# The last two up pairs product by product, both convolutions inside the first down product, activation loads first

## The chip, the cores and the metric

One NeuronCore of one Trainium2 chip. The metric is the device time of one execution in microseconds, the median of several runs. The kernel before: 1073.26 us (median of 3 runs, 1072.83 to 1077.39).

## What is computed

One decoder layer on 1024 positions of width 1024, in fp32. The change lies in its last third, the gated MLP with a causal depthwise convolution of width 3:

```python
h = rmsnorm(x, ffn_norm_g[l])
up = causal_depthwise_conv(h @ w_up[l], conv_w[l], conv_b[l])
a, bgate = jnp.split(up, [D_FF], axis=-1)
x = x + (jax.nn.silu(a) * bgate) @ w_down[l]
...
return rmsnorm(x, final_norm_g)
```

D_FF is 2816, which is 22 tiles of 128 rows for each of the two halves of `up`.

## The kernel before, in words

**Two-part numbers.** A TensorE product of an fp32 matrix is made of three: both operands are split into a high part (`...h`, made by ACT, line 113 for weights and 842 for activations of the down product) and the rest (`...l`, a subtraction on DVE, lines 114 and 843), and h·h, h·l and l·h are added up.

**Up pairs.** A `Unit` takes two column tiles of `w_up`, tile i and tile 22 + i (`wa` and `wb`; pair 20 is u20 in the trace), and computes both with seven products of half size instead of eight (Strassen's scheme in Winograd's form). Each product is 12 matmuls of 128x512 (line 146). The right-hand operands R11, R21, T1, T2, R22, T3, T4 lie split on the chip. The weights of the products are `a` (the raw tile), `b` (sums s), `c` (sums t) and `d` (half a raw tile); `prep_a`, `sums_s`, `split_s`, `sums_t`, `split_t` and `prep_b` make them (the sums: line 159), and `p(k)` issues product k and then what reads it from PSUM (`n1` to `n7`, lines 204 to 246). Products 1, 2, 5, 6, 3, 7, 4 accumulate in PSUM tiles X, Z and Y; from them come `ra` and `rb`, the pair's two rows of `up`. Product 7's sum must be read from X (`n7`, DVE) before product 4 adds to X.

**Convolution.** `conv` makes three taps for ra and three for rb (ACT for the first, lines 789 and 798 with the silu; DVE for two each, lines 790 and 791) and the gate, a product on DVE (line 800; on POOL for the first two pairs). The tiles are named cv. `blocks_of(j)` (POOL, lines 804 to 812) then writes seven combinations of the gated tiles of two pairs to `gb` in DRAM: plain copies and differences.

**Down product.** It has the same form: seven products over blocks of half size, in the order SEQ = 2, 1, 5, 6, 3, 7, 4, each over 11 tiles (22 pairs, two by two) and four row tiles p, so 4 x 33 = 132 matmuls (line 883). Product 2 goes to dZ, 1, 6 and 7 to dX, 5 and 3 to dY. `load_act(i, j)` fetches a pair of tiles from `gb` (g20 to g24 for product 2, g10 to g14 for product 1, and so on) and splits them; `load_wt(i, t)` fetches a weight tile of `w_down` (wd20 to wd25 for product 2) and splits it, for products 5, 6, 3 and 7 after a sum or difference with another. The last of the 11 tiles of products 2 and 1 does not come through `gb`: it is split from the gated tile on the chip (g2e and g1e). dZ is therefore issued without its last tile first, and with it at the end.

**What sets the order.** Engines run their instructions in order; a scheduler of the framework sets the order on each from the source's order and its own estimates. In blocks marked `manual_schedule` for PE, TensorE's order is that of the source. Raw weights of pairs and of the down product share four buffers (tag w); the split high and low parts of weights rotate over three buffers each (wh, wl). SP starts nearly all loads, POOL the stores of `gb`. Before the change, TensorE's manual block begins at dZ (line 981): the last pair, 21, runs alone by `pair(last, ahead)`, which calls the convolution of pair 20 and the loads of product 2 between its products, and the scheduler places the first matmuls of dZ between pair 21's.

Of the kernel before, what the change touches and what calls it, by code (L numbers as in the profile page):

```python
# [12 lines left out]
AF = mybir.ActivationFunctionType  # L13
ALU = mybir.AluOpType
# [3 lines left out]
S = 1024  # L18
# [5 lines left out]
FT = FF // P  # L24
# [3 lines left out]
KH = FT // 2  # L28
# [37 lines left out]
def decoder_layer(ctx, tc, io, out):  # L66
    nc = tc.nc
# [8 lines left out]
    def U(name, dt=F32, shape=(P, 1024)):  # L76
        return up.tile(list(shape), dt, tag="u", name=name)
# [21 lines left out]
    def V(key, j=None):  # L99
        o, n = VEC[key]  # L100
        return vec[:, o:o + n] if j is None else vec[:, o + j:o + j + 1]
# [49 lines left out]
    class Unit:  # L151
        def __init__(u, ws, R, name, tile=W, kh=4):
            u.wa, u.wb = ws
            u.kh = kh
            u.a = [u.wa[:, o:o + kh] for o in (0, kh)] if not isinstance(u.wa, list) else u.wa
            u.R, u.name, u.tile = R, name, tile
# [4 lines left out]
        def prep(u, src, key, eng=None):  # L161
            h, l = split_w(src, u.name + key, eng=eng)
            return [(h[:, o:o + u.kh], l[:, o:o + u.kh]) for o in range(0, src.shape[1], u.kh)]
# [105 lines left out]
    def unit(srcs, R, name):  # L269
        u = Unit(load_pair(srcs, name), R, name)  # L270
        u.prep_a()
        u.p(1)
        u.p(2)
        return finish(u)
# [11 lines left out]
    def both(us, *names):  # L286
        for n in names:
            for u in us:
                u.p(n) if isinstance(n, int) else getattr(u, n)()
# [29 lines left out]
    R = {k: [] for k in ("R11", "R21", "T1", "T2", "R22", "T3", "T4")}  # L319
# [143 lines left out]
    for half in range(2):  # L463
        ps = M(f"r1bc{half}")
# [34 lines left out]
    for h in range(NH):  # L499
# [10 lines left out]
        for half in range(2):  # L510
            ps = small4(f"pS{h}{half}", lambda o, j: nc.tensor.matmul(o, kT[:, cut(half * 4 + j)], qT[:, cut(half * 4 + j)], start=True, stop=True))
# [14 lines left out]
        for n in range(NCH - 1):  # L526
            src = pkv[n // 4][:, n % 4]
# [27 lines left out]
        g = h  # L555
        ws, cb = hc[:, 2], hc[:, 3]
# [8 lines left out]
        if g:  # L565
            svT, u = unit([io["w_in"][:, 20 + g], io["w_in"][:, 16 + g]], R, f"G{g}")
        else:
            g0.wb = W("G0w1")
            nc.sync.dma_start(g0.wb, io["w_in"][:, 16])
            svT, u = finish(g0)  # L570
# [58 lines left out]
    R = {}  # L629
# [8 lines left out]
    class Out:  # L638
# [28 lines left out]
        def all(u):  # L667
            for f in (u.product, u.residual, u.square, u.add):
                f()
# [30 lines left out]
    us = u0, u1 = [Unit(load_pair([io["w_up"][:, i], io["w_up"][:, FT + i]], f"u{i}", UW), R, f"u{i}", UW) for i in range(2)]  # L700
# [83 lines left out]
    gbs = [dp.tile([P, 7, n, HALF], F32, name=f"gb{n}") for n in (KH - 1, 1)]  # L784
    halves = lambda t: t.rearrange("p (a b) -> p a b", b=HALF)

    def taps(r, i):
        t = U(f"cv{i}")
        nc.scalar.activation(t, r, AF.Identity, scale=V("cw", 88 + i), bias=V("cb", i))
        nc.vector.scalar_tensor_tensor(t[:, 1:], r[:, :S - 1], V("cw", 44 + i), t[:, 1:], ALU.mult, ALU.add)  # L790
        nc.vector.scalar_tensor_tensor(t[:, 2:], r[:, :S - 2], V("cw", i), t[:, 2:], ALU.mult, ALU.add)  # L791
        return t

    g = {}

    def conv(ra, rb, i):
        a = taps(ra, i)
        nc.scalar.activation(a, a, AF.Silu)  # L798
        b = taps(rb, FT + i)
        (nc.gpsimd if i < 2 else nc.vector).tensor_tensor(a, a, b, ALU.mult)  # L800
        g[i] = halves(a)


    def blocks_of(j):
# [18 lines left out]
    SEQ = [2, 1, 5, 6, 3, 7, 4]  # L823
# [4 lines left out]
    act = {i: [] for i in SEQ}  # L828
# [3 lines left out]
    def load_act(i, j):  # L832
        n = min(2, KH - 2 * j)
        src = gbs[0][:, BLK[KEY[i]], 2 * j:2 * j + 2] if n == 2 else gbs[1][:, BLK[KEY[i]]]
        if n == 2:
            h, l = [U(f"g{i}{j}{x}", F32R, PAIR) for x in "hl"]
        else:
            e = U(f"g{i}{j}e", F32R, PAIR)
            h, l = e[:, :1], e[:, 1:]
        x = l.bitcast(F32)  # L840
        nc.sync.dma_start(x, src)
        nc.scalar.activation(h, x, AF.Copy)
        nc.vector.tensor_tensor(l, x, h.bitcast(F32), ALU.subtract)
        act[i] += [(h[:, m], l[:, m]) for m in range(n)]
# [8 lines left out]
    def load_wt(i, t):  # L853
        lo, n = 8 * t, min(8, NB - 8 * t)
        raw = []
        for m, src in enumerate(SRC[i]):
            raw.append(W(f"wd{i}{t}{m}")[:, :n])
            nc.sync.dma_start(raw[-1], src[:, lo:lo + n])
        w = raw[0]
        if i == 5:  # L860
            sums[t] = U(f"ds{t}", F32, (P, 8, P))
        if i in (5, 6, 3):
            s = sums[t][:, :n]
            x, y, op = {5: (w, raw[-1], ALU.add), 6: (s, w, ALU.subtract), 3: (w, s, ALU.subtract)}[i]
            nc.vector.tensor_tensor(s, x, y, op)  # L865
            w = s
        elif i == 7:
            nc.vector.tensor_tensor(w, w, raw[1], ALU.subtract)  # L868
        h, l = split_w(w, f"wd{i}{t}", tile=(lambda name: U(name, F32R, (P, 8, P))) if i == 2 and t % 2 == 0 or i == SEQ[-1] and t < 4 else None)
        wts[i] += [(h[:, m], l[:, m]) for m in range(n)]  # L870
# [3 lines left out]
    def load_x2(n):  # L874
        x2[n] = U(f"x2{n}")
        nc.sync.dma_start(x2[n], x2d[:, n])

    def down(ps, i, p, start, ks, stop, cols=slice(0, HALF)):
        first = start
        todo = [(k, s) for k in ks for s in range(2)] + [(k, 2) for k in ks]  # L880
        for n, (k, s) in enumerate(todo):
            w, r = wts[i][p * KH + k], act[i][k]
            nc.tensor.matmul(ps, w[s // 2], r[s % 2][:, cols], start=first, stop=stop and n == len(todo) - 1, skip_group_check=True)  # L883
            first = False

    def acc(n, half, ps):
        o = hs(x2[n], half)
        nc.vector.tensor_tensor(o, ps, o, ALU.add)  # L888

    PREP = {2: [(load_act, j) for j in range(5)]}  # L890
    for i in SEQ[1:]:
        PREP[i] = [(f, int(j)) for f, j in zip([load_act, load_act, load_wt] * 3 + [load_wt] * 3, "010231452345")]
        if i == 1:
            PREP[i] = [f for f in PREP[i] if f != (load_act, 5)]

    def prep(i, n):
        for f, j in PREP[i][:n]:
            f(i, j)
        PREP[i] = PREP[i][n:]


    def pair(u, ahead):
        u.p(1)
        ahead(1)
        u.p(2)
        u.sums_s(nc.gpsimd)
        u.split_s()
        ahead(2)
        u.p(5)
        ahead(3)  # L910
        u.p(6)
        u.sums_t(nc.gpsimd)
        u.split_t()
        ahead(4)
        u.p(3)
        u.prep_b()
        ahead(5)
        u.p(7)
        ahead(6)
        u.p(4)  # L920

    for i, (ra, rb) in enumerate(early):
        conv(ra, rb, i)
# [4 lines left out]
        if i % 2:  # L928
            blocks_of(i // 2)

    held = unit([io["w_up"][:, FT - 2], io["w_up"][:, 2 * FT - 2]], R, f"u{FT - 2}")
    last = Up(FT - 1)

    def ahead(j):
        if j == 1:
            conv(*held, FT - 2)
        if j < 6:
            prep(2, 1)
        if j > 2:
            load_wt(2, j - 3)  # L940

    pair(last, ahead)
    for t in range(4, 6):
        load_wt(2, t)
    prep(1, 2)
    conv(last.ra, last.rb, FT - 1)
    load_x2(0)
    load_x2(2)
    e, o = g[FT - 2], g[FT - 1]
# [1 line left out]
    last1 = U("g1e", F32R, PAIR)  # L951
# [26 lines left out]

    ba, bb, bc = Block(HALF, HALF), Block(0, 256), Block(256, 256)
    X = [None] * 4  # L980
    with tc.manual_schedule(engines={mybir.EngineType.PE}):
        Z = [M(f"dZ{p}") for p in range(3)] + [A("dZ3")]
        for p in range(4):
            down(Z[p], 2, p, True, range(KH - 1), False)
            prep(1, 1)
        for p in range(4):
            down(Z[p], 2, p, False, [KH - 1], True)
            if p:
                load_x2(2 * p + 2) if p < 3 else None
            acc(2 * p, 0, Z[p])  # L990
        prep(1, 20)
        act[1].append((last1[:, 0], last1[:, 1]))
        for i, nxt in zip(SEQ[1:-1], SEQ[2:]):
            for p in range(4):
                prep(nxt, 3)
                if i in (1, 6, 7):
                    if i == 1:
                        X[p] = A(f"dX{p}")
                    ps = X[p]
                else:  # L1000
                    if i == 5:
                        load_x2(2 * p + 1)
                    ps = M(f"dY{i}{p}")
                down(ps, i, p, i in (1, 5, 3), range(KH), True)
                for n, half in {1: [(0, 0)], 5: [(0, 1), (1, 1)], 6: [(0, 1)], 3: [(0, 1)], 7: [(1, 1)]}[i]:
                    acc(2 * p + n, half, ps)
                if i == 7:
                    for b in (ba, bb, bc):
                        b.square(2 * p)

    with tc.manual_schedule(engines={mybir.EngineType.PE, mybir.EngineType.DVE, mybir.EngineType.Activation}):
        def squares(b, ns):
# [7 lines left out]
        for k in range(8):  # L1020
            s, p = divmod(k, 4)
# [55 lines left out]
```

## Time and profile before

| | |
|---|---|
| median of 3 runs | 1073.26 us (1072.83 to 1077.39) |
| the profiled execution | 1072.93 us, of which the span is 1071.2 us |
| TensorE busy | 1027.7 us, 96% of the span |
| DVE busy | 826.4 us, 77% |
| ACT busy | 490.7 us, 46% |
| POOL busy | 206.8 us, 19% |
| loads and stores | 141.58 MB, mean 132 GB/s |

A view called the chain follows the execution back from its last instruction, at each step to what released it. The waits say who waited for whom. A timeline lists instructions with their start, their duration and, in brackets, the idle time of the engine before them and what ended it. The windows give busy time per engine, the clock granted to TensorE as a share of full speed, and what the DMA engines did. PE is TensorE's matmuls, DVE VectorE, ACT ScalarE, POOL GpSimd, SP SyncE; buffer numbers are left out of names.

### The profile page before, as it was taken

Reading aid. Unit: us, or ns where it says so; the run is one execution under the profiler, and the core shown is the slowest. Engines: PE = TensorE matmul, PEld = TensorE weight load, DVE = VectorE, ACT = ScalarE, POOL = GpSimd, SP = SyncE. Lnnn points to the kernel's source line nnn. Section 1 sums busy time; section 2 is a strip of 40 time slices with the busy share of each in tenths; the row PEclk is TensorE's granted clock in tenths of the full one; section 3 lists DMA queues with packets and bytes.
Section 4 is the critical chain, followed back from the end, with each engine's and each line's share of the span. In section 5 each row is a group of like instructions: output and inputs, shape, how many; then the busy total and the mean of one; then the engine's idle time right before and its main releaser. Section 6 shows DMA issues by size and latency. Waiting matters only on the chain.

```text
span 1071.2 us, 12690 instructions
## 1 busy us (share of the span) xinstructions
PE 1027.7 (96%) x4794; PEld 849.4 (79%) x4794; DVE 826.4 (77%) x998; ACT 490.7 (46%) x690; POOL 206.8 (19%) x145
## 2 busy tenths in 40 slices
PE   7798999999999999989999999999998899999996
PEld 5586888888888888768888888888887778878896
DVE  7868886958867478998887878878786587886565
ACT  6653444334364353654444534544445444344440
POOL 4602330412210000061123023032123130000000
PEclk9899999999999999999999999999999999999998
DMA  7251031121365240022333233233235678974614
GB/s 286 80 196 40 22 110 62 52 77 62 99 222 191 98 157 20 20 103 98 104 108 103 86 128 118 61 116 119 81 116 177 216 284 296 365 240 161 198 57 158
DMA packets 48446, 141.58 MB, mean 132 GB/s; under 512 B 5056, under 2 KB 9536, under 8 KB 48384
## 3 DMA queue, kind: packets, MB, share of 16 engines
q1 hardware_dynamic: 42752, 120.58, 33.5%
q0 software_dynamic: 5632, 20.19, 4.8%
q8 instruction: 37, 0.61, 0.2%
q14 instruction: 25, 0.20, 0.1%
HBM read 109.03 MB, written 31.72 MB: 131 GB/s over the span
## 4 chain that ended last, share of the span: by engine, by line
PE 73%; DVE 14%; issue 5%; ACT 4%; DMA 2%; POOL 1%; SPq 0%; DVEq 0%; ACTq 0%
PE dX L883 10%; PE po L135 8%; PE dY L883 6%; DVE cv L791 2%; PE A0X L146 2%; PE B0X L146 1%; PE G1X L146 1%; PE A3X L146 1%; PE B3X L146 1%; PE u4X L146 1%; PE u20X L146 1%; DVE cv L790 1%; PE G0X L146 1%; PE B1X L146 1%; DMA wd<-in_w_down 1%
## 5 line engine op out<-in xcount | busy, mean ns | idle before, releaser
L798 ACT ACTIVATE cv<-cv 128x1024 f32<-128x1024 f32 x22 | 23.4, 1062 | 73.5 <-DVE cv L791 73.5
L810 POOL TENSOR_TENSOR cv<-cv 128x512 f32<-128x512 f32 x22 | 38.5, 1752 | 20.8 <-DMA gb<-cv 18.8
L808 POOL DMA_DIRECT2D gb<-cv x11 | 7.9, 715 | 151.0 <-DVE cv L800 150.7
L800 POOL TENSOR_TENSOR cv<-cv,cv 128x1024 f32<-128x1024 f32 x2 | 7.7, 3874 | 140.4 <-ACT u2p L227 140.4
L810 POOL TENSOR_TENSOR cv<-cv,cv 128x512 f32<-128x512 f32 x22 | 31.7, 1442 | 4.8 <-DMA gb<-cv 3.3
L807 POOL DMA_DIRECT2D gb<-cv x11 | 6.5, 589 | 113.8 <-DVE cv L800 113.5
L655 DVE TENSOR_TENSOR xr<-po,xr 128x512 f32<-128x512 f32 x16 | 10.8, 688 | 20.0 <-PE po L135 18.7
L965 ACT ACTIVATE x3q<-x 128x256 f32<-128x256 f32 (+1 forms) x21 | 9.3, 483 | 33.6 <-DVE x L1026 28.3
L800 DVE TENSOR_TENSOR cv<-cv,cv 128x1024 f32<-128x1024 f32 x20 | 24.3, 1216 | 0.1
L661 ACT ACTIVATE xq<-xr 128x512 f32<-128x512 f32 x14 | 8.8, 628 | 24.2 <-DVE xr L655 17.1
L546 ACT ACTIVATE sT<-po 128x128 f32<-128x128 f32 x32 | 8.4, 277 | 13.3 <-PE po L538 13.2
L868 DVE TENSOR_TENSOR wd<-wd,wd 128x1024 f32<-128x1024 f32 (+1 forms) x6 | 6.8, 1136 | 9.7 <-DMA wd<-in_w_down 9.7
L967 DVE TENSOR_TENSOR sq<-sq,x3q 128x256 f32<-128x256 f32 (+1 forms) x20 | 9.8, 516 | 4.2 <-ACT x3q L965 3.8
L976 DVE SCALAR_TENSOR_TENSOR x<-x,vec,r 128x256 f32<-128x256 f32 (+1 forms) x24 | 12.0, 564 | 1.3 <-PE r L622 1.3
L665 DVE TENSOR_TENSOR sq<-sq,xq 128x512 f32<-128x512 f32 x13 | 8.9, 688 | 3.2 <-ACT xq L661 3.1
L675 ACT ACTIVATE nx<-xr,vec 128x512 f32<-128x512 f32 x16 | 10.8, 708 | 0.0
L509 ACT ACTIVATE kn<-pk,vec 128x512 f32<-128x512 f32 x8 | 5.2, 680 | 11.8 <-PE pk L508 11.8
L1026 DVE TENSOR_TENSOR x<-dX,x 128x256 f32<-128x256 f32 x8 | 3.4, 424 | 8.5 <-PE dX L883 8.5
L678 DVE TENSOR_TENSOR nx<-nx,r 128x1024 f32<-128x1024 f32 x8 | 9.5, 1216 | 0.4 <-PE r L622 0.4
L865 DVE TENSOR_TENSOR ds<-wd,wd 128x1024 f32<-128x1024 f32 (+1 forms) x6 | 6.8, 1134 | 3.4 <-DMA wd<-in_w_down 3.4
L336 POOL TENSOR_SCALAR x<-x,vec 128x512 f32<-128x512 f32 x4 | 8.0, 2004 | 7.1 <-DVE R110l L330 7.1
L888 DVE TENSOR_TENSOR x<-dY,x 128x512 f32<-128x512 f32 x12 | 8.1, 685 | 1.1 <-DMA x<-x2d 1.1
(5708 smaller groups left out, 3854.3 us busy)
## 6 DMA issues: line engine op xcount, KB each, us to landing
wd<-in_w_down SPq DMA_DIRECT2D x45, 512.0 KB, 4.4
gb<-cv POOLq DMA_DIRECT2D x33, 512.0 KB, 3.2
wo<-in_w_out SPq DMA_DIRECT2D x10, 512.0 KB, 3.8
x<-in_xT SPq DMA_DIRECT2D x8, 512.0 KB, 8.9
xn<-in_xN SPq DMA_DIRECT2D x8, 512.0 KB, 5.5
xr<-in_xT SPq DMA_DIRECT2D x8, 512.0 KB, 5.9
x2d<-xr SPq DMA_DIRECT2D x8, 512.0 KB, 3.2
x<-x2d SPq DMA_DIRECT2D x8, 512.0 KB, 5.3
```

Of the source, the lines that this page charges most:

```text
L135: nc.tensor.matmul(ps, a, b, start=(k == 0 and t == 0), stop=(k == n - 1 and t == 2))
L146: nc.tensor.matmul(ps, a[:, k], b, start=(start and i == 0), stop=(i == 3 * n - 1), skip_group_check=not start)
L655: nc.vector.tensor_tensor(u.y, u.ps, u.y, ALU.add)
L675: nc.scalar.activation(nx[n // 2][:, n % 2], xr[th][n // 2][:, n % 2], AF.Identity, scale=V("g2", n))
L790: nc.vector.scalar_tensor_tensor(t[:, 1:], r[:, :S - 1], V("cw", 44 + i), t[:, 1:], ALU.mult, ALU.add)
L791: nc.vector.scalar_tensor_tensor(t[:, 2:], r[:, :S - 2], V("cw", i), t[:, 2:], ALU.mult, ALU.add)
L798: nc.scalar.activation(a, a, AF.Silu)
L800: (nc.gpsimd if i < 2 else nc.vector).tensor_tensor(a, a, b, ALU.mult)
L810: nc.gpsimd.tensor_tensor(x, y, z, ALU.subtract)
L883: nc.tensor.matmul(ps, w[s // 2], r[s % 2][:, cols], start=first, stop=stop and n == len(todo) - 1, skip_group_check=True)
L967: nc.vector.tensor_tensor(sq[:, u.blk], sq[:, u.blk], u.t, ALU.add)
L976: nc.vector.scalar_tensor_tensor(y, y, V("gf", n), u.nr.rs, ALU.mult, ALU.mult)
```

## The change

Pairs 20 and 21 are made together: each step is issued for both, one product of the one behind the same product of the other. Their sums s and t go to DVE (before, those of pair 21 were on POOL) and into tiles of the large pool. Both convolutions are called after the last product, so that they lie beside dZ, and TensorE's order is set by hand from pair 20's first product on. The five loads g20 to g24 are started by POOL instead of SP. For product 1 all five activation loads come before its six weight loads; before, each weight followed two activations. The classes and helpers that `taps` is cut into do the same work as before for every other pair.

```diff
+    class Taps:
+        def last(u):
+            u.t = U(f"cv{u.i}")
+            nc.scalar.activation(u.t, u.r, AF.Identity, scale=V("cw", 88 + u.i), bias=V("cb", u.i))
+        def tap(u, d):
+            nc.vector.scalar_tensor_tensor(u.t[:, d:], u.r[:, :S - d], V("cw", 88 - 44 * d + u.i), u.t[:, d:], ALU.mult, ALU.add)
...
     def conv(ra, rb, i):
...
+        a = Taps(ra, i).all()
+        silu(a)
+        gate(i, a, Taps(rb, FT + i).all(), nc.gpsimd if i < 2 else None)
...
-        nc.sync.dma_start(x, src)
+        (nc.gpsimd if i == SEQ[0] else nc.sync).dma_start(x, src)
...
         if i == 1:
-            PREP[i] = [f for f in PREP[i] if f != (load_act, 5)]
+            PREP[i] = [(load_act, j) for j in range(5)] + [(load_wt, j) for j in range(6)]
...
-    held = unit([io["w_up"][:, FT - 2], io["w_up"][:, 2 * FT - 2]], R, f"u{FT - 2}")
-    last = Up(FT - 1)
...
-    pair(last, ahead)
-    for t in range(4, 6):
-        load_wt(2, t)
-    prep(1, 2)
-    conv(last.ra, last.rb, FT - 1)
+    manual = ExitStack()
+    manual.enter_context(tc.manual_schedule(engines={mybir.EngineType.PE}))
+    us = [Up(i) for i in (FT - 2, FT - 1)]
+    for u in us:
+        u.tile = UW
+        u.p(1)
+    both(us, "sums_s", "split_s", 2, "sums_t")
+    prep(2, 1)
+    both(us, 5)
+    prep(2, 1)
+    both(us, "split_t", 6)
+    prep(2, 1)
+    both(us, 3)
+    load_wt(2, 0)
+    prep(2, 1)
+    both(us, 7, "prep_b")
+    prep(2, 1)
+    load_wt(2, 1)
+    both(us, 4)
+    load_wt(2, 2)
+    for i, u in enumerate(us):
+        conv(u.ra, u.rb, FT - 2 + i)
+        load_wt(2, 3 + i)
+        prep(1, 1)
+    load_wt(2, 5)
+    prep(1, 3)
```

What this makes of the engines' lists, at three places.

On ACT, around the first splits for the down product (g2xh and wd2xh are high parts of dZ's operands, u20p and u21p evictions of products, u21ch and u21dh the last operands of pair 21). Before:

```order
L220 ACTIVATE u21p_6222<-u21Y 128x512
L842 ACTIVATE g20h<-g20l 128x1024
L227 ACTIVATE u21p_6247<-u21X 128x512
L842 ACTIVATE g21h<-g21l 128x1024
L842 ACTIVATE g22h<-g22l 128x1024
L113 ACTIVATE wd20h<-wd_6229 128x1024
L842 ACTIVATE g23h<-g23l 128x1024
L113 ACTIVATE u21ch<-u21t 128x1024
```

And now:

```order
L113 ACTIVATE u21ch<-u21t 128x1024
L227 ACTIVATE u20p_6177<-u20X 128x512
L113 ACTIVATE u20dh<-u20w_6022 128x512
L227 ACTIVATE u21p_6191<-u21X 128x512
L857 ACTIVATE g22h<-g22l 128x1024
L113 ACTIVATE wd20h<-wd_6224 128x1024
L857 ACTIVATE g23h<-g23l 128x1024
L113 ACTIVATE u21dh<-u21w_6030 128x512
L113 ACTIVATE wd21h<-wd_6276 128x1024
```

u21ch stood behind four splits for dZ and now stands ahead of g22h and wd20h; u21dh stands directly behind g23h.

On POOL, behind the first store and difference of pairs 18 and 19 (cv_5866 is pair 18's gated tile, cv_6001 pair 19's). Now:

```order
L856 DMA g20l<-gb_3525 128x1024
L856 DMA g21l<-gb_3525 128x1024
L856 DMA g22l<-gb_3525 128x1024
L823 DMA gb_3525<-cv_6001 128x2x512
L825 TENSOR_TENSOR cv_5866<-cv_6001,cv_5866 128x512
L826 DMA gb_3525<-cv_5866 128x2x512
L825 TENSOR_TENSOR cv_6001<-cv_6001,cv_5866 128x512
L856 DMA g23l<-gb_3525 128x1024
L825 TENSOR_TENSOR cv_6001<-cv_6001 128x512
L827 DMA gb_3525<-cv_6001 128x2x512
L856 DMA g24l<-gb_3525 128x1024
```

The five loads have come in from SP's list, three ahead of pair 19's stores and two among them; the four sums for u21s and u21t, which stood here before, have gone to DVE.

On TensorE, from the first half of pair 20's product 1 (R110, R111 and so on are the halves of R11). Now:

```order
L146 MATMUL u20X<-R111h,u20al 128x512 x2
L146 MATMUL u21X<-R110h,u21ah 128x512
L146 MATMUL u21X<-R110l,u21ah 128x512
L146 MATMUL u21X<-R110h,u21ah 128x512
L146 MATMUL u21X<-R110l,u21ah 128x512
L146 MATMUL u21X<-R111h,u21ah 128x512
```

Pair 21's first product stands directly behind pair 20's; before, pair 20's products Z and Y came here and u21X followed the 84th matmul. From there the list goes on in blocks of twelve, first pair 20, then pair 21, for products 2, 5, 6, 3, 7 and 4, and then all 132 of dZ.

## Rows read from the trace of the kernel before

**Rows 1.** The page's chain that ended last: share of the span by engine.

```profile
PE 73%; DVE 14%; issue 5%; ACT 4%; DMA 2%; POOL 1%; SPq 0%; DVEq 0%; ACTq 0%
```

**Rows 2.** Waits of PE, 780 to 960: us in total, times, longest.

```profile
PE dZ L883 <- ACT wd20h L113: 3.5, 1, 3.5
PE u21Y L146 <- ACT u21ch L113: 2.5, 1, 2.5
PE dX L883 <- DVE g65e L843: 1.5, 1, 1.5
PE dX L883 <- DVE g14l L843: 0.9, 1, 0.9
```

**Rows 3.** Windows: length, busy us (instructions), granted clock, DMA share, GB/s.

```profile
827.10:830.65 3.55, 0.03 (x1) 1.00 0.01 2
830.65:836.40 5.75, 5.71 (x16) 0.70 0.12 46
836.40:838.85 2.45, 0.00 (x1) 1.00 0.49 129
...
910.00:930.00 20.00, 20.00 (x90) 16.57 (x89) 17.44 (x19) 6.88 (x7) 0.00 (x0) 1.00 0.93 346
```

**Rows 4.** Timeline of PE: start, duration, instruction, idle before and releaser.

```profile
791.61 0.39 PE L146 MATMUL u20X<-R110h,u20ah 128*128 128x512 f32 x1
...
810.65 0.39 PE L146 MATMUL u21X<-R110h,u21ah 128*128 128x512 f32 x1
...
873.42 0.39 PE L883 MATMUL dX<-g10h,wd10h 128*128 128x512 f32 x1
...
877.05 0.39 PE L883 MATMUL dX<-g14h,wd11h 128*128 128x512 f32 x1
878.36 0.50 PE L883 MATMUL dX<-g14l,wd11h 128*128 128x512 f32 x1 [0.92 <-DVE g14l L843]
```

**Rows 5.** Timeline of ACT.

```profile
829.55 1.04 ACT L113 ACTIVATE wd20h<-wd 128x1024 fp32r<-128x1024 f32 x1
...
837.74 1.06 ACT L113 ACTIVATE u21ch<-u21t 128x1024 fp32r<-128x1024 f32 x1 [6.20 <-POOL u21t L159]
...
857.46 1.23 ACT L789 ACTIVATE cv<-u21ra,vec 128x1024 f32<-128x1024 f32 x1
```

**Rows 6.** Timeline of POOL.

```profile
811.70 0.72 POOL L808 DMA_DIRECT2D gb<-cv  x1 [6.23 <-DVE cv L800]
...
817.11 1.93 POOL L810 TENSOR_TENSOR cv<-cv,cv 128x512 f32<-128x512 f32 x1 [2.34 <-DMA gb<-cv]
...
821.55 0.72 POOL L812 DMA_DIRECT2D gb<-cv  x1 [0.30 <-POOL cv L810]
...
834.29 2.20 POOL L159 TENSOR_TENSOR u21t<-u21w,u21s 128x512 f32<-128x512 f32 x1 [2.62 <-DVE wd20l L114]
```

**Rows 7.** Timeline of DVE.

```profile
817.80 2.31 DVE L790 SCALAR_TENSOR_TENSOR cv<-u20ra,vec,cv 128x1023 f32<-128x1023 f32 x1
...
825.45 1.28 DVE L790 SCALAR_TENSOR_TENSOR cv<-u20rb,vec,cv 128x1023 f32<-128x1023 f32 x1 [3.11 <-ACT cv L789]
...
831.85 1.22 DVE L843 TENSOR_TENSOR g22l<-g22l,g22h 128x1024 fp32r<-128x1024 f32 x1
...
933.84 1.22 DVE L114 TENSOR_TENSOR wd61l<-ds,wd61h 128x1024 fp32r<-128x1024 f32 x1 [0.86 <-PE dY L883]
...
940.12 0.68 DVE L843 TENSOR_TENSOR g65e<-g65e 128x512 fp32r<-128x512 f32 x1
```

**Rows 8.** DMA issues, 770 to 945: issuing queue, count, size, median us to landing.

```profile
wd<-in_w_down SPq DMA_DIRECT2D x31, 512.0 KB, 4.5
gb<-cv POOLq DMA_DIRECT2D x9, 512.0 KB, 3.8
...
g24l<-gb SPq DMA_DIRECT2D x1, 512.0 KB, 7.7
...
g13l<-gb SPq DMA_DIRECT2D x1, 512.0 KB, 8.3
```

More of the change, by code (lines that the diff above doesn't have):

```diff
@@ L785, in decoder_layer, with __init__, all, silu @@
     halves = lambda t: t.rearrange("p (a b) -> p a b", b=HALF)
[L787 to L792, printed above, removed]
+    class Taps:
+        def __init__(u, r, i):
+            u.r, u.i = r, i
+        def last(u):
[3 more added lines that the diff above has]
+            nc.vector.scalar_tensor_tensor(u.t[:, d:], u.r[:, :S - d], V("cw", 88 - 44 * d + u.i), u.t[:, d:], ALU.mult, ALU.add)
+        def all(u):
+            u.last()
+            u.tap(1)
+            u.tap(2)
+            return u.t
+    def silu(t):
+        nc.scalar.activation(t, t, AF.Silu)
+    def gate(i, a, b, eng=None):
+        (eng or nc.vector).tensor_tensor(a, a, b, ALU.mult)
+        g[i] = halves(a)
     g = {}
     def conv(ra, rb, i):
[L797 to L801, printed above, removed]
+        a = Taps(ra, i).all()
+        silu(a)
+        gate(i, a, Taps(rb, FT + i).all(), nc.gpsimd if i < 2 else None)
     def blocks_of(j):
@@ L899, in prep @@
         PREP[i] = PREP[i][n:]
[L902 to L920, printed above, removed]
     for i, (ra, rb) in enumerate(early):
@@ L929, in decoder_layer @@
             blocks_of(i // 2)
-    held = unit([io["w_up"][:, FT - 2], io["w_up"][:, 2 * FT - 2]], R, f"u{FT - 2}")
-    last = Up(FT - 1)
[L934 to L940, printed above, removed]
-    pair(last, ahead)
-    for t in range(4, 6):
-        load_wt(2, t)
-    prep(1, 2)
-    conv(last.ra, last.rb, FT - 1)
+    manual = ExitStack()
[24 more added lines that the diff above has]
+    prep(1, 3)
     load_x2(0)
@@ L980, in decoder_layer @@
     X = [None] * 4
-    with tc.manual_schedule(engines={mybir.EngineType.PE}):
-        Z = [M(f"dZ{p}") for p in range(3)] + [A("dZ3")]
-        for p in range(4):
[L984 to L1009, printed above, removed]
@@ new lines, in decoder_layer @@
+    Z = [M(f"dZ{p}") for p in range(3)] + [A("dZ3")]
+    for p in range(4):
+        down(Z[p], 2, p, True, range(KH - 1), False)
+        prep(1, 1)
+    for p in range(4):
+        down(Z[p], 2, p, False, [KH - 1], True)
+        if p:
+            load_x2(2 * p + 2) if p < 3 else None
+        acc(2 * p, 0, Z[p])
+    prep(1, 20)
+    act[1].append((last1[:, 0], last1[:, 1]))
+    for i, nxt in zip(SEQ[1:-1], SEQ[2:]):
+        for p in range(4):
+            prep(nxt, 3)
+            if i in (1, 6, 7):
+                if i == 1:
+                    X[p] = A(f"dX{p}")
+                ps = X[p]
+            else:
+                if i == 5:
+                    load_x2(2 * p + 1)
+                ps = M(f"dY{i}{p}")
+            down(ps, i, p, i in (1, 5, 3), range(KH), True)
+            for n, half in {1: [(0, 0)], 5: [(0, 1), (1, 1)], 6: [(0, 1)], 3: [(0, 1)], 7: [(1, 1)]}[i]:
+                acc(2 * p + n, half, ps)
+            if i == 7:
+                for b in (ba, bb, bc):
+                    b.square(2 * p)
@@ L1011, in decoder_layer @@
+    manual.close()
     with tc.manual_schedule(engines={mybir.EngineType.PE, mybir.EngineType.DVE, mybir.EngineType.Activation}):
```

## The prediction

> **What bounds the kernel now.** I read the chain of waits first: 73% of it is PE [rows 1], so the kernel is TensorE-bound and only moments in which TensorE stands still, or runs slowly, can be won. Next I asked who made TensorE wait between the last up pairs and the down products [rows 2]: four stops, for wd20h (3.5 us), u21ch (2.5), g65e (1.5) and g14l (0.9). The timeline around them shows what follows a stop. After the first one TensorE ran the 16 matmuls of dZ between 830.65 and 836.40 at a mean granted clock of 0.70, part of them at the 1.2 GHz level; in the stretches before and after it had 1.00 [rows 3]. Undisturbed, one matmul takes 0.2267 us: 84 of them stand between the first of u20X at 791.61 and the first of u21X at 810.65 [rows 4], and 19.04 / 84 = 0.2267.
>
> Why it stopped: ACT is an in-order engine and reached wd20h at 829.55 only, because g20h, g21h and g22h stood ahead of it and behind u21's evictions [rows 5]. The second stop is a chain: POOL started u21t at 834.29 (it had waited 2.62 us for wd20l, whose raw tile gave up the buffer), ACT waited 6.2 us for it and split it at 837.74 [rows 5, 6]. Pair 21 alone could not fill TensorE while its own operands were made; that is the hole that the down product was pulled into, half ready.
>
> **The change, part by part.**
>
> *TensorE's list.* From the first u20X matmul to the first dX matmul the same 324 matmuls are issued, in another order: 24 of pair 19, 168 of pairs 20 and 21, 132 of dZ. Before, this took 791.61 to 873.42, 81.81 us [rows 4]. Without a stop it takes 324 x 0.2267 = 73.45 us and dX begins at 865.06: **8.4 us earlier**. As a cross-check, the stops of 3.52 and 2.5 us and the slow stretch (16 matmuls in about 5.7 us instead of 3.6) make 8.1; restarts are the rest. So the question is whether each operand is ready by 791.61 + n x 0.2267, n being its place in the new list. Up to u20X all lists but a few DVE sums are the same, so I start from before's times and follow each engine's new order, with steps from rows: DVE about 1.2 us for a convolution tap, 1.14 for a 128x1024 subtract and 0.6 for a half one, ACT 1.0 for a split and 1.15 for the biased activation [rows 5, 7] (rows overlap the next by nearly 0.1).
>
> - u21ah, n = 24, needed 797.1. It takes the buffer of u19c's high half, free after the eighth matmul of u19's product 7, at 795.4; ready 796.5.
> - u20bh and u21bl, n = 72 and 92, needed 807.9 and 812.5. The four sums of s run on DVE after pair 19's taps and end at 803.0; ACT splits at 805.4 and 806.3; DVE finishes u21bl at 809.7. Slack 2.5 and 2.8.
> - u20cl and u21cl, n = 128 and 140, needed 820.6 and 823.4. The sums t end at 812.7, the lows at 816.2 and 818.5. POOL's block subtractions run beside them, and a DVE tap beside POOL took 2.31 us instead of 1.28 [rows 7]; with two such meetings 817.4 and 820.3. Slack 3.
> - u20rb and u21rb, needed 829.7 and 832.4: each hangs on its own product 7, done one product earlier (827.3 and 830.0), plus 0.6 on DVE. Slack about 1.8.
> - u21dh, n = 180, needed 832.4. On ACT it now stands right behind g23h, and g23l is fetched by POOL: its queue waits for pair 19's gate on DVE (813.9), stores, subtracts, stores, waits for the first store (5.4 us from issue to the next subtraction, as 811.70 to 817.11 before) and subtracts again for 1.9 [rows 6]; g23l is issued at 821.3. POOL's own DMAs landed in 3.8 us, the slowest of the five loads on SP's queue took 7.7 [rows 8]: 825.1 to 829.0. I take 3.8, as it is the row for this queue. u21dh is then ready at 827.1 (831 at the far end). Slack 5, at worst 1.4.
> - g24h, n = 208, needed 838.8: issued about 825.2, landed 829 to 833; ACT reaches it at 833.5 behind u20rb. Ready 834.5.
> - The weights: SP no longer carries the five g2 loads, but the raw tiles of the weights take the buffers of the pairs' raw weights. wd20 is issued at 811.6, wd22 at 819.7, wd24 at 829.6, wd25 at 831.7; with landings of 4.5 us [rows 8] all come before or at ACT's turn. I cost them at nothing.
> - g2e, n = 312, needed 862.3: both convolutions, eight taps of 1.2, two gates and nine splits, go through DVE between 834.5 and 860.0. Before, one convolution stood outside. They are covered by 27 us of dZ. With g13l landing as slowly as before (8.3 us [rows 8]), g2e is ready at 861.3. Slack 2.3 down to 1.0: the tightest place.
>
> So I cost the moved sums (four x 0.6 = 2.4 us more on DVE, less on POOL) and the five DMA issues on POOL (0.72 each [rows 6]) at nothing; what hides them is that pair 20 now runs while pair 21's operands are made, and the reverse.
>
> *Activations of product 1 ahead of its weights.* g14l was late: the interval from g14h to the next matmul was 878.36 - 877.05 = 1.31 instead of 0.23 [rows 4], and the next ones were 0.1 slow: 1.2 us. Now g14 is issued about 848.4, four transfers ahead of its old place; at 8.3 us it is split by 859.4, and dX wants it at 868.7. **1.2 us** more. Its weights wd11 and wd12 are on the chip by then; their splits wait for dZ's last matmuls to free buffers, as before.
>
> *The stop for g65e.* DVE's order there is unchanged. Its run of work starts at 933.84 with wd61l, which waited for TensorE (releaser: dY), and reaches g65e at 940.12 [rows 7]. A chain that starts at TensorE moves with TensorE, so I count **0** here, with a gain of up to 1.6 left for the range.
>
> **Sum.** 8.4 + 1.2 = 9.6 us. The profiled execution took 1072.93 us, of which 1071.2 is the span: 1063.3. The median of the runs is 0.33 higher, so I predict 1073.26 - 9.6 = **1063.7 us**. About 0.5%, 5.4 us, is what a measurement of this kernel can tell from no change: 1067.9 is the border.
>
> **Rivals.**
> 1. *One feed late in the pairs or at g2e.* The slacks of 1 to 3 us are the ends of chains of some thirty steps, each a few hundredths uncertain. For it: DVE is doubled by POOL in places, and DVE and ACT serve two pairs in turn. Against it: most feeds hang on TensorE's own products one product back, and slip with it. A miss of 1 to 4 us, with some matmuls at the lower clock if it is as long as the 3.5 us stop, gives 1065 to 1069; middle 1066.5.
> 2. *Transfers take the gain.* Between 910 and 930 the DMA engines are 93% busy at 346 GB/s [rows 3]. If the loads of products 5 and 6 kept their old times, TensorE would arrive 9.6 us early and wait 9.6 longer: 1073. Against it: those loads are released by DVE splits that wait for TensorE, so they start about 9 to 10 us earlier too, and g50 and g51, 1 MB, are out of the way before. I give 1071 for a mostly lost gain.
> 3. *POOL's loads are late* (the slower case). ACT stands at g23h until POOL's load has landed, with u21dh, wd21h and u20's eviction behind it. TensorE stops for L - 9.5 us, if L is the time from issue at 821.3 to landing (821.3 + L + 1.6 against 832.4), and 2 us follow at the lower clock as after the 3.5 us stop. It decides from L = 17: then 9.6 are gone. At L = 24 the time is 1063.7 + 14.5 + 2.1 = 1080. Against it: 3.8 us measured for this queue. Its issues, at 811.70 and 821.55, took 0.72 us [rows 6].
>
> The Trainium skill, page "SBUF — State Buffer", section "A bandwidth-pool intuition that's wrong", warns of that: a DMA issued by GpSimd takes about 620 ns alone and about 3100 ns beside a DVE copy that holds the port which the two share. The issues of 0.72 us here, while DVE ran its taps, do not show it. If it held for the three issues up to g23l, an estimate from that page's figures puts POOL 7 us later, u21dh near 834 and the time near 1065.5, which lies in the range as it is.
>
> That the change does not do what it says is excluded by the order: TensorE's list is side by side, in blocks of twelve.
>
> **How the numbers follow.** Forecast 0.70, rival 1 0.15, rival 2 0.10, rival 3 0.05. The forecast's own spread is 1061.0 (the stop for g65e goes as well, 1.6, and a little) to 1065. With rival 1 up to 1067.6 that holds 0.8. Faster by over 0.5% (under 1067.9): 0.70 + 0.12 of rival 1 = 0.82. Within: 0.03 + 0.09 = 0.12. Slower by over 0.5%: rival 3 and a tenth of rival 2, 0.06.
>
> **What would show it.** Right: TensorE without a stop from u20X to the last dZ, granted clock 1.00 throughout, about 73.5 us from the first u20X to the first dX; ACT's g23h before 827 and u21dh before 832; no wait for g14l; the wait for g65e still near 1.5. Wrong: a wait of TensorE for u21dh, wd or g2e; a wait over 5 us at g65e or in dY (transfers); POOL issues over 2 us.

## The result, and the profile after

The changed kernel took 1066.89 us (median of 11 runs, 1063.00 to 1070.71), the kernel before beside it 1073.37 (11 runs, 1071.54 to 1077.39): a ratio of 0.9939 (95% interval 0.9921 to 0.9958), 6.5 us faster. The forecast was 1063.7, 9.6 us faster; the result lies in the range of 1061.0 to 1067.6, 3.2 us above the forecast and outside the forecast's own spread, which ended at 1065. The same two kernels were compared twice more (e1 and e11 below, on two different chips), with medians that differ by 9.2 and 11.3 us, so the three comparisons average 9.0.

The profiled execution took 1066.89 us, its span is 1065.1. The chain that ended last, of the changed kernel's page, answers to [rows 1]:

```profile
PE 75%; DVE 11%; issue 4%; ACT 3%; POOL 0%; DMA 0%; DVEq 0%; ACTq 0%
```

The waits of PE between 780 and 960 answer to [rows 2]. Of four stops one is left, the one that the prediction left standing (the 0.2 us for u19p were there before, too):

```profile
PE dX L898 <- DVE g65e L858: 1.5, 1, 1.5
PE u19Y L146 <- ACT u19p L220: 0.2, 1, 0.2
```

The windows answer to [rows 3]. The columns are the length, the busy us and instructions of PE, of PEld (TensorE's weight loads), of DVE, ACT and POOL, then the granted clock, the DMA share and GB/s. The first window is the two pairs with the last 24 matmuls of pair 19, the second dZ, the third dX, the last the stretch around the stop for g65e:

```profile
794.87:838.39 43.52, 43.52 (x194) 36.04 (x192) 35.67 (x38) 22.68 (x28) 14.46 (x13) 1.00 0.51 170
838.39:868.31 29.92, 29.92 (x134) 24.77 (x132) 25.08 (x25) 16.82 (x20) 5.80 (x7) 1.00 0.82 306
868.31:898.23 29.92, 29.92 (x134) 24.77 (x132) 22.03 (x22) 12.47 (x13) 1.54 (x2) 1.00 0.74 262
925.00:940.00 15.00, 13.54 (x60) 10.90 (x59) 13.91 (x16) 6.05 (x7) 0.00 (x0) 1.00 0.93 351
```

PE is busy in every microsecond of the first three, at a granted clock of 1.00, where the 16 matmuls of dZ had 0.70 before. In PE's timeline the first matmuls of the stages, and of g14, answer to [rows 4]:

```profile
794.87 0.39 PE L146 MATMUL u20X<-R110h,u20ah 128*128 128x512 f32 x1
...
838.39 0.39 PE L898 MATMUL dZ<-g20h,wd20h 128*128 128x512 f32 x1
...
868.31 0.39 PE L898 MATMUL dX<-g10h,wd10h 128*128 128x512 f32 x1
...
871.93 0.39 PE L898 MATMUL dX<-g14h,wd11h 128*128 128x512 f32 x1
872.16 0.39 PE L898 MATMUL dX<-g14l,wd11h 128*128 128x512 f32 x1
...
898.23 0.39 PE L898 MATMUL dY<-g50h,wd50h 128*128 128x512 f32 x1
...
934.53 0.50 PE L898 MATMUL dX<-g65e,wd61h 128*128 128x512 f32 x1 [1.47 <-DVE g65e L858]
```

From the first u20X to the first dX it is 868.31 - 794.87 = 73.44 us (81.81 before); g14l follows g14h by 0.23 instead of 1.31. But u20X begins at 794.87 and not at 791.61 [rows 4]: 3.26 us went before the change has its first matmul, in code that it leaves as it was but for pair 20's sums, which DVE made there before.

All profiles, the experiments' too, read in the same way (span less the start of dY is the last column but one):

| kernel | u20X starts | u20X to dX | dX to dY | dY to end | span |
|---|---|---|---|---|---|
| before | 791.61 | 81.81 | 31.13 | 166.65 | 1071.2 |
| before again (e2) | 792.17 | 83.29 | 30.90 | 169.74 | 1076.1 |
| before, acts first (e3) | 791.18 | 81.83 | 30.83 | 166.96 | 1070.8 |
| before, sums on DVE (e10) | 792.41 | 80.33 | 30.81 | 169.44 | 1073.0 |
| changed | 794.87 | 73.44 | 29.92 | 166.87 | 1065.1 |
| changed again (e1) | 793.07 | 73.44 | 29.92 | 167.08 | 1063.5 |
| changed, third (e11) | 791.62 | 73.44 | 29.92 | 166.32 | 1061.3 |
| acts between (e5) | 793.72 | 73.44 | 29.92 | 167.02 | 1064.1 |
| loads on SP (e4) | 791.68 | 73.44 | 29.92 | 166.36 | 1061.4 |
| loads on SP again (e12) | 790.98 | 73.44 | 29.92 | 171.16 | 1065.5 |
| PE by scheduler (e7) | 792.05 | 73.65 | 29.92 | 166.88 | 1062.5 |
| sums on POOL (e6) | 792.82 | 83.55 | 29.92 | 167.21 | 1073.5 |
| g65 third (e8) | 792.44 | 73.44 | 29.92 | 170.20 | 1066.0 |
| g64, g65 ahead (e9) | 790.89 | 73.44 | 29.92 | 169.45 | 1063.7 |

### The profile page after: what moved, and what is told of

It reads as the page before. It is cut to its first block, busy times and chain, and to the rows that moved or that the text cites. A ratio compares the mean times of both kernels' runs of the same rounds, so it can differ in the third digit from the quotient of the medians.

```text
span 1065.1 us, 12682 instructions
## 1 busy us (share of the span) xinstructions
PE 1027.6 (96%) x4794; PEld 849.0 (80%) x4794; DVE 829.6 (78%) x1002; ACT 490.2 (46%) x690; POOL 200.7 (19%) x146
## 4 chain that ended last, share of the span: by engine, by line
PE 75%; DVE 11%; issue 4%; ACT 3%; POOL 0%; DMA 0%; DVEq 0%; ACTq 0%
PE dX L898 11%; PE po L135 8%; PE dY L898 6%; PE dZ L898 3%; DVE cv L796 2%; PE G1X L146 1%; PE A3X L146 1%; PE B3X L146 1%; PE u4X L146 1%; PE u21X L146 1%; PE u20X L146 1%; PE u18X L146 1%; PE B1X L146 1%; PE G2X L146 1%; PE G3X L146 1%
## 5 line engine op out<-in xcount | busy, mean ns | idle before, releaser
L825 POOL TENSOR_TENSOR cv<-cv 128x512 f32<-128x512 f32 x22 | 36.3, 1650 | 25.3 <-DMA gb<-cv 19.3
```

The costliest lines, as they stand in the source:

```text
L825: nc.gpsimd.tensor_tensor(x, y, z, ALU.subtract)
```

## The experiments

**The same kernels again: e1, e2, e11.** No edit.

> The changed kernel once more, nothing edited. In the first profile of it TensorE took 270.2 us from the first matmul of u20X to the end, 9.3 us less than before (279.55), yet began u20X 3.3 us later (794.88 against 791.61), in code that the change does not touch. Theory A: the length of that opening differs from execution to execution of one and the same program (arrival of the first loads, pace of the first chains). Then this profile shows 270.2 within 0.5 from u20X on, and u20X may begin anywhere between 790 and 797. Theory B: the changed program makes the opening longer each time. Then u20X begins at 794.5 to 795.5 again, and again the wait for B0bh is about 5.4 us where before it was 1.8.

> The kernel before once more, nothing edited. Theory A (the opening varies by execution): 279.5 us within 0.7 from the first matmul of u20X to the end, and a start of u20X that may be off 791.61 by as much as 3 us. Theory B (the opening belongs to the program): u20X begins at 791.6 within 0.5 again, with a wait of 1.8 us for B0bh.

> The changed kernel a third time, nothing edited, beside the two before it and the one after it. Expected from the stages: 9.2 to 9.6 us faster than the kernel before, ratio 0.991 within its interval; start of u20X anywhere from 790.9 to 794.9, and 270.2 to 270.5 us from there to the end.

e1: median 1064.78 against 1073.94, ratio 0.9911 (0.9895 to 0.9927). e11: 1064.22 against 1075.49, 0.9895 (0.9880 to 0.9910). e2: one run of 1077.90. Theory A holds as far as these runs go: the changed kernel began u20X at 794.87, 793.07 and 791.62. Over all 14 profiles, whose code is alike up to there but for pair 20's sums, the start lies between 790.89 and 794.87; the four with the old pairs average 791.8, the ten with the new ones 792.4, which is less apart than two profiles of one kernel. A part of it may be the chip and not the execution: e1, e2, e5 and e8 ran on one chip, e4, e6, e7 and e9 on a second, e3, e10, e11 and e12 on a third, and on each of them the four starts lie within 1.4 to 1.9 us. No program was profiled twice on a chip that the record names. In the opening the difference shows at the first matmul that needs B0bh; the first row is of the changed kernel's first profile, the second of its third (PE's timeline):

```profile
36.66 0.79 PE L146 MATMUL B0Y<-T10h,B0bh 128*128 128x512 f32 x1 [5.40 <-ACT B0bh L113]
```

```profile
30.81 0.50 PE L146 MATMUL B0Y<-T10h,B0bh 128*128 128x512 f32 x1 [2.18 <-ACT B0bh L113]
```

PE waited 5.40 us there in one execution and 2.18 in the other (3.87 in e1). The third profile loses a part of its lead again, 2.2 us at B0bl and 3.0 at T20l, and is 3.25 ahead at u20X. What makes the first chains slower or faster is open.

e2 misses its 279.5 us from u20X on: it has 283.9, as its stretch took 83.29 and its stops for g65e and g64l were 2.3 and 0.5. The kernel before is not a fixed yardstick either. e11 missed both of its figures a little: 269.7 us from u20X to the end, where 270.2 to 270.5 were expected, and 11.3 us between the medians, where 9.2 to 9.6 were.

**The activations of product 1: e5 and e3.** e5 is the changed kernel with the old list:

```diff
-            PREP[i] = [(load_act, j) for j in range(5)] + [(load_wt, j) for j in range(6)]
+            PREP[i] = [f for f in PREP[i] if f != (load_act, 5)]
```

> The changed kernel with the activations of product 1 back among its weights. My theory: g14 is then issued four transfers later, and the stop in front of dX's tenth k comes back: 31.1 us from the first matmul of dX to the first of dY instead of 29.9, 1.2 us in all, so 1.2 us slower than the changed kernel. Rival: the stop before was there only since dZ was torn by its own stops and the loads were bunched; with the pairs side by side g14 lands in time in either order: 29.9 and no difference. A second rival: the order of loads moves the stop, so that another operand of dX is late by 1 us or more.

e3 puts the reverse of this edit, alone, into the kernel before.

> The kernel before with one thing changed: the activations of product 1 are listed ahead of its weights. The stop for g14l (0.9 us; 31.1 and 30.9 us from the first matmul of dX to the first of dY) was to go by this part of the change, 1.2 us by the prediction. In the changed kernel with the old list the stop did not come back (29.92), g14 being issued at 851.92 instead of 851.13. Theory now: the list decides little; what held g14 back is SP's queue, which stood 11.9 us for a weight buffer that the late split of wd10 freed, and here two x2 loads alone (0.85 us) move behind g14. So 30.2 to 31.1 us for dX to dY, a gain of 0 to 0.9. Rival, the prediction's step: 29.9, a gain of 1.2, from this part alone.

In both, the prediction's step fell. With the old list the changed kernel still has 29.92 us from dX to dY and no stop for g14l; with the new list alone the kernel before has 30.83 (30.90 and 31.13 without) and a stop of 0.6. SP's queue says why. First e5, then e3, then the changed kernel and the kernel before:

```profile
849.82 0.33 SPq L873 DMA_DIRECT2D wd<-in_w_down  x1
850.25 0.37 SPq L856 DMA_DIRECT2D g13l<-gb  x1
850.72 1.04 SPq L891 DMA_DIRECT2D x<-x2d  x2
851.92 0.32 SPq L856 DMA_DIRECT2D g14l<-gb  x1
860.17 0.33 SPq L873 DMA_DIRECT2D wd<-in_w_down  x1
```

```profile
868.62 0.33 SPq L858 DMA_DIRECT2D wd<-in_w_down  x1
869.12 0.32 SPq L841 DMA_DIRECT2D g14l<-gb  x1
869.53 0.85 SPq L876 DMA_DIRECT2D x<-x2d  x2
```

```profile
851.13 0.32 SPq L856 DMA_DIRECT2D g14l<-gb  x1
...
860.67 0.33 SPq L873 DMA_DIRECT2D wd<-in_w_down  x1
```

```profile
868.12 0.33 SPq L858 DMA_DIRECT2D wd<-in_w_down  x1
...
869.57 0.32 SPq L841 DMA_DIRECT2D g14l<-gb  x1
```

g14 is issued either ahead of the weight load that waits for a buffer (released by the split of wd10; the queue stood for it 11.9 us before, 12.3 in e3, 7.9 in e5), or behind it. The kernel's list is only what the scheduler starts from: with pairs side by side it places g14 ahead of that load under both lists, in the old program behind it under both. So the 1.2 us in dX do not come from the list. With the five loads back on SP (e4), the sums on POOL (e6) or TensorE's order left to the scheduler (e7), each alone, dX keeps its 29.92 too; what is left are the rearranged pairs and convolutions, by exclusion and not by a run of their own.

The medians do not fit this: e5 had 1067.91, ratio 0.9935 (0.9920 to 0.9951), 3.1 us above e1 of the same comparison, and e3 had the ratio 0.9972 (0.9958 to 0.9987), 3.0 us faster than before where 0 to 0.9 were expected, both as if the list were worth 3 us. The one profile of e5, of the fastest of its six runs, shows none of it in dX, that of e3 0.1 to 0.3. Where the rest comes from is open: the list is shown to do next to nothing in dX, and no more.

**Who makes the sums: e6 and e10.** In e6 the sums s and t of both pairs go to POOL, eight operations:

```diff
-    both(us, "sums_s", "split_s", 2, "sums_t")
+    for u in us:
+        u.sums_s(nc.gpsimd)
+    both(us, "split_s", 2)
+    for u in us:
+        u.sums_t(nc.gpsimd)
```

> The changed kernel with the four sums s and t of the last two pairs on POOL, as pair 21 had them before, instead of DVE. My theory, by which these sums cost nothing on DVE and would not gain on POOL: DVE gives up 4 x 0.6 = 2.4 us, the feeds u20bh to u21cl have 2.5 to 3 us of slack, POOL takes 1 to 2 us for each; 73.4 us from the first matmul of u20X to the first of dX within 0.5, and no difference in time. Rival: POOL, in order, has the sums t behind the waits for its loads, and the splits of c come late as they did for pair 21 before: a stop of 1 to 4 us for u20ch or u21ch, 75 to 78 us for the stretch.

Median 1076.07, ratio 0.9992 (0.9977 to 1.0007): the whole gain is gone. The theory fell, and the rival, which had priced it at 1.6 to 4.6 us (75 to 78 for the stretch) and named u20ch or u21ch, was too mild and not at the right operand. But e6 goes further than the change back: before, only pair 21's four operations were on POOL, and DVE had made pair 20's between 784.7 and 788.9. The changed kernel with pair 21's sums alone on POOL was not run. Waits of PE in e6, 780 to 960:

```profile
PE u20Y L146 <- DVE u20bl L114: 4.2, 1, 4.2
PE u20X L146 <- DVE u20rb L159: 2.2, 1, 2.2
PE dX L898 <- DVE g65e L858: 1.5, 1, 1.5
```

In e6 POOL's timeline, then DVE's:

```profile
804.98 1.28 POOL L159 TENSOR_TENSOR u21s<-u21s,u21w 128x512 f32<-128x512 f32 x1
806.23 1.29 POOL L159 TENSOR_TENSOR u20t<-u20w,u20s 128x512 f32<-128x512 f32 x1
807.49 2.28 POOL L159 TENSOR_TENSOR u20t<-u20w,u20w 128x512 f32<-128x512 f32 x1
```

```profile
799.33 4.54 DVE L796 SCALAR_TENSOR_TENSOR cv<-u19ra,vec,cv 128x1023 f32<-128x1023 f32 x2
807.16 1.45 DVE L796 SCALAR_TENSOR_TENSOR cv<-u19rb,vec,cv 128x1023 f32<-128x1023 f32 x1 [3.29 <-ACT cv L793]
...
809.13 1.71 DVE L796 SCALAR_TENSOR_TENSOR cv<-u19rb,vec,cv 128x1022 f32<-128x1022 f32 x1
810.88 2.18 DVE L808 TENSOR_TENSOR cv<-cv,cv 128x1024 f32<-128x1024 f32 x1
812.98 2.28 DVE L114 TENSOR_TENSOR u20bl<-u20s,u20bh 128x1024 fp32r<-128x1024 f32 x1
```

and two of these operations of DVE in the changed kernel:

```profile
801.36 2.59 DVE L796 SCALAR_TENSOR_TENSOR cv<-u19ra,vec,cv 128x1023 f32<-128x1023 f32 x2
...
809.51 1.22 DVE L114 TENSOR_TENSOR u20bl<-u20s,u20bh 128x1024 fp32r<-128x1024 f32 x1
```

A sum on POOL takes 1.28 where DVE stands idle and 2.28 where DVE works; two taps of DVE take 4.54 instead of 2.59. The scheduler's order changed as well: in e6 a tap and the gate, 3.85 us together, stand ahead of u20bl on DVE, which in the changed kernel come behind it. That is more than half of the 6.6 us by which u20bl ends later, counted from u20X's start. u20bl, whose slack was 2.3, so came 4.2 late, and after the stop PE had a mean granted clock of 0.78 in this window of e6:

```profile
812.00:818.00 6.00, 2.68 (x6) 2.15 (x7) 6.00 (x5) 0.57 (x1) 5.68 (x6) 0.78 0.57 162
```

The Trainium skill, page "SBUF — State Buffer", section "SBUF: two separate sides", describes a port pair shared by DVE and GpSimd: when a DVE instruction has two SBUF inputs and the GpSimd one reads SBUF, the one that starts first has the pair for its whole instruction, and the other waits. That a sum grows from 1.28 to 2.28 us, by less than one whole operation of DVE (1.2), agrees in kind. In the changed kernel a difference of the same size on POOL took far longer, beside three subtractions of DVE that kept their 1.22 (POOL's row, then the first of the three):

```profile
818.24 4.65 POOL L825 TENSOR_TENSOR cv<-cv,cv 128x512 f32<-128x512 f32 x1
```

```profile
818.25 1.22 DVE L114 TENSOR_TENSOR u20cl<-u20t,u20ch 128x1024 fp32r<-128x1024 f32 x1
```

So the rows show that the two engines slow each other, and not what decides which of them waits.

e10 makes the counterpart in the kernel before, sums of pair 21 on DVE:

```diff
-        u.sums_s(nc.gpsimd)
+        u.sums_s()
...
-        u.sums_t(nc.gpsimd)
+        u.sums_t()
```

> The kernel before with one thing changed: the sums s and t of pair 21 are made on DVE instead of POOL, as the changed kernel makes them for both pairs. In the changed kernel with the sums on POOL the gain was gone: 83.55 us from the first matmul of u20X to the first of dX instead of 73.44, as POOL and DVE slowed each other (DVE's taps 2.3 us instead of 1.2, POOL's sums 2.3 instead of 1.3) and u20bl came 4.2 us late. Theory: the move of the sums and the order side by side are needed together; pair 21 alone cannot fill TensorE while its operands are made, so the stop of 3.5 us for wd20h stays and that for u21ch shrinks: 78 to 81 us for the stretch (81.81 and 83.29 in the two profiles of the kernel before), 1 to 3 us faster than before. Rival: the sums on POOL were the whole cause of the hole, and 74 to 75 us come out without any reordering, 7 to 8 us faster.

1073.12 against 1075.49, ratio 0.9975 (0.9962 to 0.9987): 2.7 us by the ratio (1.4 to 4.1). The stretch is 80.33, 1.5 us shorter than in the first profile of before; the stop for u21ch went from 2.5 to 1.2, that for wd20h stayed at 3.5. The theory holds: the sums alone give 1.5, the order side by side with all eight operations on POOL loses 1.7 (83.55), both together give 8.4.

**PE's order and POOL's queue: e7, e4, e12.** e7 enters the hand-fixed order at dZ only:

```diff
-    manual = ExitStack()
-    manual.enter_context(tc.manual_schedule(engines={mybir.EngineType.PE}))
     us = [Up(i) for i in (FT - 2, FT - 1)]
...
     X = [None] * 4
+    manual = ExitStack()
+    manual.enter_context(tc.manual_schedule(engines={mybir.EngineType.PE}))
```

> The changed kernel with TensorE's order inside the two pairs left to the scheduler; it mixes the twelves of neighbouring products (it starts u20Z ahead of pair 19's product 3, for one). My theory, by which it is the second pair's work that fills TensorE while operands are made, whatever the exact order: 73.4 us from the first matmul of u20X to the first of dX, within 1 us. Rival: the scheduler puts matmuls where its own estimate has their operands ready; where the chip is later, TensorE, in order, stops: one stop or more of 1 to 4 us, 75 to 78 us for the stretch, and the fixed order is a part of the gain.

73.65 us, 0.2 more, and 1064.73, ratio 0.9881 (0.9858 to 0.9903): the fixed order of twelves is worth 0.2 us in this profile. With e10 this leaves the second pair's work beside the first, and the convolutions behind both, as what fills PE; no run separates these two.

```diff
-        (nc.gpsimd if i == SEQ[0] else nc.sync).dma_start(x, src)
+        nc.sync.dma_start(x, src)
```

> The changed kernel with the five loads of g2 issued by SP again instead of POOL. My theory, by which the queue that issues them is worth nothing as long as each load lands before its matmul: 73.4 us from the first matmul of u20X to the first of dX, within 0.5, and the same time as the changed kernel; g23l may land earlier or later than 830.6 by 3 us, its slack. Rival: SP is an in-order queue, and a weight load that waits for a buffer holds g22l, g23l or g24l back (or the reverse): TensorE stops for 1 to 5 us at u21dh, g23 or a weight of product 2, and the stretch takes 75 to 79 us.

> The changed kernel with the five loads of g2 on SP once more, beside the changed kernel on the same chip. In the first run it had 73.44 us for the pairs and dZ as the changed kernel has, a stop of 1.7 us for g65e, a median of 1063.47 us and the ratio 0.9872. Theory: the queue is worth nothing, the stages are the same and the difference came from the opening and from the runs of that chip: within 1 us of the changed kernel beside it. Rival: POOL's issues cost something outside TensorE's stops: 2 us faster than the changed kernel or more.

e4 had 1063.47, ratio 0.9872 (0.9850 to 0.9895); e12, beside e11, 1065.41 and 0.9910 (0.9893 to 0.9927), where the unedited kernel had 1064.22. The stretch is 73.44 in both. So the queue is worth nothing in the stage, and e4's low median did not come again: e12 was 1.2 us slower than the kernel beside it, a little more than the 1 us expected, with runs that overlap. On SP g23l is issued 21.8 us behind u20X's start in e4 instead of 30.3, and nothing needs it sooner.

**The stop that is left: e8 and e9.** Both reorder the loads of product 6, e8 first, then e9. In e8's diff one part is left out here: the split activations are kept by number, so that TensorE still takes them in their old order.

```diff
+        if i == 6:
+            PREP[i] = [(f, int(j)) for f, j in zip([load_act, load_act, load_wt] * 3 + [load_wt] * 3, "010521342345")]
```

> The changed kernel with the sixth load of product 6's activations (g65) brought and split as the third of them. In the changed kernel TensorE still stops once in this part, 1.5 us for g65e, the last of a run of work of DVE that starts when TensorE frees a buffer. Theory: the stop belongs to the place of g65 in DVE's order; moved ahead, it goes, 1.5 us faster than the changed kernel, about 168.4 to 165.4 from the first matmul of dY on. Rival: DVE's run of work is as long as before and only its last piece changes name, so that TensorE waits as long for g63, g64 or a weight: within 0.3 us of the changed kernel.

```diff
+        if i == 6:
+            PREP[i] = [(load_act, 0), (load_act, 1), (load_wt, 0)] + [(load_act, j) for j in range(2, 6)] + [(load_wt, j) for j in range(1, 6)]
```

> The changed kernel with the loads g64 and g65 of product 6 issued right behind g63, ahead of the weights wd61 and wd62 (activations stay in the order of their use). In the changed kernel SP issued g63 at 913.62 and g64 at 922.76: between them stood two weight loads that waited 5.2 us for a buffer which DVE frees, and TensorE stood 1.5 us for g65e; putting g65 third, in the earlier run, made g64 later and the stops 3.4 us. Theory: the stop comes from SP's queue, where the loads wait behind a weight load that has no buffer yet. Then g64 is issued by 916, g65e is split before 931, the stop goes, and from the first matmul of dY to the end 165.4 us pass instead of 166.9 to 167.1: 1.5 us faster. Rival: the transfers are full there (DMA 0.84 to 0.9 busy), so what g64 and g65 win the weights lose: a stop of 1 us or more for wd61, wd62 or g30, and no gain.

e8: 1065.42 where e1 had 1064.78, and two stops of 1.7 us for g64h and g64l; the changed name of the late piece was the rival's, its price was higher. e9: 1067.56, ratio 0.9904 (0.9881 to 0.9927), stops of 1.7 and 0.4 for g65e. SP's queue in e9, and its window:

```profile
911.42 0.64 SPq L856 DMA_DIRECT2D g63l<-gb  x1
914.68 4.59 SPq L873 DMA_DIRECT2D wd<-in_w_down  x2
919.36 0.38 SPq L856 DMA_DIRECT2D g64l<-gb  x1
...
922.66 0.42 SPq L856 DMA_DIRECT2D g65e<-gb  x1
```

```profile
920.00:930.00 10.00, 9.36 (x41) 7.19 (x39) 7.89 (x10) 4.53 (x6) 0.00 (x0) 1.00 0.98 353
```

Two weight loads that wait for buffers still stand between g63 and g64. The scheduler left the queue as it was but for one load of x2: g64 is issued 128.5 us behind u20X's start, in the changed kernel 127.9 (922.76). The DMA engines are 98% busy in that window. Theory and rival are not told apart by it, since the loads were not moved past the wait; neither version gained.

## Why the prediction came out as it did

**TensorE's list: right.** 73.45 us were forecast from u20X to dX, 73.44 measured, in all three profiles of the changed kernel. The two stops and the stretch at the lower clock are gone.

**The feeds: right, none was late.** Slack in the changed kernel, from the end of the operation to the first matmul that reads it (forecast in brackets): u21ah 0.6 (0.6), u20bh 2.6 (2.5), u21bl 2.7 (2.8), u20cl 4.4 (4.4, or 3 beside POOL), u20rb 1.8 (1.8), u21dh 3.4 (5, at worst 1.4), g24h 4.5 (4.3), g2e 3.2 (2.3 down to 1.0). u20bl, which the prediction did not price, had 2.3. u21dh lost 1.6, as g23l took 5.4 us to land and not 3.8 (a row of POOL's stores, not of loads), and ACT stood for it:

```profile
825.20 0.57 POOL L856 DMA_DIRECT2D g23l<-gb  x1
```

```profile
830.65 1.06 ACT L857 ACTIVATE g23h<-g23l 128x1024 fp32r<-128x1024 f32 x1 [5.89 <-DMA g23l<-gb]
831.62 0.61 ACT L113 ACTIVATE u21dh<-u21w 128x512 fp32r<-128x512 f32 x1
```

So one sign of being right did not come: g23h was to start before 827 and started at 830.65, 827.4 with the 3.26 us of the opening taken off. POOL's issues of g2 took 0.53 to 0.58 us and the loads landed in 3.4 to 6.5, far from the 17 of the slower case (rival 3). Of the two issues of 0.72 us that the prediction names as beside DVE's taps, only the one at 821.55 was [rows 6, 7].

**The moved sums: the cost right, the account too short.** "Costed at nothing" holds for DVE. But the prediction treated their move as a cost to be hidden. e6 shows that with both pairs' sums on POOL the gain is nil, and e10 that the move alone shortens the stretch by 1.5 us; what the changed kernel would lose with pair 21's alone on POOL is not shown.

**Product 1's activations: right in size, wrong in cause.** 31.13 to 29.92 is 1.21 us, 1.2 was forecast; e5 and e3 show that the new list is not what gives it. The number came true by luck.

**The stop for g65e: right.** 1.5 in the first profiles of both kernels, though it differs by execution: 2.3 in e2, 2.1 in e1, 1.5 in e11. Rival 2's lost gain did not come: u20X to the end shrank by 9.4 us (279.59 to 270.23), and the loads of the later products started earlier too (g50 was issued at 853.91 instead of 875.29, g60 at 898.83 instead of 904.87).

**The step that failed**, though the result lies in the range, is "Up to u20X all lists but a few DVE sums are the same, so I start from before's times". The lists are the same, the times are not: in the profiled execution u20X came 3.26 us later. The spans differ by 1071.2 - 1065.1 = 6.1 us, and that is 8.37 (u20X to dX) + 1.21 (dX to dY) - 0.22 (dY to the end) - 3.26. The profile of before happened to have an early start (791.61), and the prediction took one execution's opening as given. It put no such spread into the forecast's own range either: only rival 1, a late feed, carried the range from 1065 to 1067.6, and a feed was not what was late. That the result lies in the range is luck to that extent. That the median of the 11 runs lies higher for the same reason was not shown; their spread of 7.7 us is wider than that of the opening alone. The stages that the change touches gave 9.4 us, and the three comparisons on average 9.0, so 9.6 was nearly right for the change.

## What to carry to other kernels

In this kernel a pair that makes its own operands left holes in TensorE's work; a second, equal pair in step beside it, with the convolutions behind both, filled them, and the exact order of TensorE's matmuls mattered little. The engine that makes the operands counts as much: with both pairs' sums on POOL, beside a busy DVE, the whole gain was lost. A list in the source is not the order in a queue: look there for what a reordering has moved. When stages are compared, take differences from one profile's own marks (first matmul to first matmul), and allow the stretch ahead of the change the spread that repeated profiles of one kernel show.

## What the runs showed that was not expected

The opening of one and the same program differed by 3.25 us between two profiles (794.87 and 791.62), half of the gain measured in the first comparison; they come from different runs and perhaps different chips, and the cause is open.

A stop near g65e costs very different amounts. e11 and e12, with equal code there, in the window 925 to 940:

```profile
925.00:940.00 15.00, 13.54 (x60) 10.90 (x59) 13.54 (x15) 5.89 (x8) 0.00 (x0) 1.00 0.78 275
```

```profile
925.00:940.00 15.00, 11.86 (x39) 8.88 (x38) 12.98 (x15) 5.28 (x6) 0.00 (x0) 0.77 0.85 315
```

e11 stopped for 1.5 us and kept a granted clock of 1.00; e12 stopped for 0.9 and 2.3 us, part of the matmuls behind ran at the 1.2 GHz level, and dY to the end took 171.16 instead of 166.32: 1.7 us more of standing, 4.8 us more time. A single stop of 2.3 us went without a fall of the clock in e3 (166.96) and with one in e10 (169.44; a granted clock of 0.66 between 940 and 945).
